# The down product of a two-layer trunk's MLP: eight quarter products feature-major, or seven token-major by Strassen's algorithm

## The chip, the cores and the metric

The kernel runs on one core of one Trainium2 chip. The metric is the device time of one execution in microseconds. Three runs of the kernel before took 1536.81 us (median), from 1536.06 to 1536.86 us.

## The reference

A trunk of two layers works on 512 positions of 1024 features, in float32. Layer 0 mixes the positions by a gated delta rule, layer 1 by a conformer convolution. Each layer then attends to a memory of 256 rows and ends with the MLP that the change concerns:

```
def sq_relu_mlp(h, w_up, w_down):
    return jnp.square(jax.nn.relu(h @ w_up)) @ w_down
```

`h` is the residual stream after `rms_norm` (each row multiplied by 1/rms and by a gain per feature). `w_up` is 1024 x 4096 and `w_down` 4096 x 1024. The result is added to the residual stream. A last `rms_norm` gives the output, 512 x 1024. Since relu is positively homogeneous, multiplying a row of `h` by 1/rms multiplies its row of the hidden activation, after the square, by 1/rms squared.

## The kernel before

Nearly all of its work is dense products on TensorE (PE). A float32 operand is split into a rounded part and the rest, and a product becomes three matmuls: rounded by rounded, rest by rounded, rounded by rest. `mm3` (L229 to L231) issues them. Weights arrive by one queue of SP (`wload`, L196) in tiles of 128 x 1024 called `raw`. `wsplit` makes `wh` by a cast on ACT (L207) and `wl` by a subtraction on DVE (L70 is the line of the helper `tt`, L73 that of `stt`, so that all such operations carry these lines). Those of `w_pw1` and half of layer 1's K and V are subtracted on POOL instead.

The activations lie feature-major: 128 features on the partitions, 512 tokens along a row. So a weight block of 128 x 128 is the stationary operand and 512 tokens move past it. One **unit** makes 128 output features: eight blocks of the inner dimension, three matmuls each, 24 matmuls in one PSUM bank.

The MLP (`mlp`, L960 on) cuts the 4096 hidden rows into four **groups** of 1024 (g = 0 to 3). A group has eight up units and eight down units. `MLP_ORDER` runs them as up 0, up 1, down 0, up 2, down 1, up 3, down 2, down 3, so that a down product never follows directly on its own up product, but for the last. After an up unit, `up_ev` has DVE take relu times 1/rms out of PSUM (`rl`; `rb` is 1/rms spread over the partitions, made by two matmuls, L300), ACT squares it (L970), and ACT and DVE split it (`uh`, `ul`). After a down unit DVE adds the bank to the residual stream (`h`). At the end of layer 0, group 3's additions are followed by the parts of the next norm: ACT multiplies by the gain (`xh`, L314), DVE makes the rest (`xl`), ACT squares, POOL sums the squares.

The last group of layer 1 is made otherwise, in `finish` (L1374 to L1396): token-major, with hidden activations as the stationary operand and 512 columns of weights moving. Four transposes per bank (L1374) bring the residual stream in.

The program is written as one list. A scheduler places each instruction on its engine by its place in that list and by when its inputs and a free tile are expected. The weight tiles come from three pools of three (`raw`, `wh`, `wl`), other wide tiles from pools `fs` and `cv`, and 512-wide tiles from one pool of 69.

Of the kernel before, what the change touches and what calls it, by code (L numbers as in the profile page):

```python
# [11 lines left out]
ALU = mybir.AluOpType  # L12
# [26 lines left out]
def tile_trunk(ctx, tc, xT, memT, prm_d, adt_d, bdw_d, tap_d, fin_d, w_ab, w_kq, w_v, w_z, w_dno, w_pw1, w_pw2,  # L39
# [5 lines left out]
    wp = ctx.enter_context(tc.tile_pool(name="wp", bufs=2))  # L45
    fsp = ctx.enter_context(tc.tile_pool(name="fsp", bufs=3))
# [10 lines left out]
    def slot(dt=F32, s="u", shape=(P, NT)):  # L57
        return up.tile(list(shape), dt, tag="u", name=nm(s))

# [46 lines left out]
    raw0 = wp.tile([P, 1024], F32, tag="raw", name="raw0", bufs=NRAW)  # L106
# [32 lines left out]
    order, srcs = [], {}  # L139

    def plan(key, src, n=2):
        srcs[key] = src
        for hf in range(n):
            order.append((key, hf))
# [14 lines left out]
    def plan_mlp(layer, last=False):  # L159
        for kind, g in MLP_ORDER:  # L160
            if last and (kind, g) == ("dn", 3):
                break
            for i in range(4):
                plan((kind, layer, g * 4 + i), (w_up if kind == "up" else w_dn)[layer, g * 4 + i])
# [11 lines left out]
    for i in range(8):  # L176
        srcs[("pw1", i)] = w_pw1[i]
        srcs[("K", 1, i) if i < 4 else ("V", 1, i - 4)] = w_k[1, i] if i < 4 else w_vv[1, i - 4]
    for kind, i in CONV_SEQ:
        if kind == "p":  # L180
            order.append((("pw1", i // 2), i % 2))
        elif kind == "k":
            order.append((("K", 1, i // 2) if i < 8 else ("V", 1, i // 2 - 4), i % 2))
# [3 lines left out]
    plan_mlp(1, True)  # L187
# [3 lines left out]
    def wload():  # L191
        u = ws["load"]
        key, hf = order[u]
        ws["load"] += 1
        raw = wp.tile([P, 1024], F32, tag="raw", name=nm("raw"), bufs=NRAW)
        nc.sync.dma_start(out=raw, in_=srcs[key][:, hf * 1024:(hf + 1) * 1024])  # L196
        ws["raw"][u] = raw

    def wsplit():
        u = ws["split"]  # L200
        ws["split"] += 1
        while ws["load"] <= u:
            wload()
        raw = ws["raw"].pop(u)
        h = wp.tile([P, 1024], F32R, tag="wh", name=nm("wh"), bufs=NW)
        lo = wp.tile([P, 1024], F32R, tag="wl", name=nm("wl"), bufs=NW)
# [3 lines left out]
        (kind, i, *j), hf = order[u]  # L210
        gp = kind == "pw1" or j and kind in "KV" and i == 1 and hf == 0
        ins.append(tt(pool if gp else dve, lo, raw, h.bitcast(F32), ALU.subtract))
        if u < 4:
            tc.keep_in_program_order(ins[1])
        ws["hl"][u] = (h, lo)

    def wnext(key, hf):
        i = ws["next"]
        assert order[i] == (key, hf), (order[i], key, hf)
        while ws["load"] < min(i + NRAW + 2, len(order)):  # L220
            wload()
        while ws["split"] < min(i + (NW if i else 1), len(order)):
            wsplit()
# [79 lines left out]
    class Norm:  # L303
        def __init__(self, gname, eng=None, two=True):
            self.eng, self.two = eng or pool, two
            self.g, self.acc, self.xs, self.n = gname, None, [], 0
# [5 lines left out]
        def parts(self, t, h):  # L312
# [4 lines left out]
            self.xs.append((xh, xl))  # L317
# [10 lines left out]
        def stat(self):  # L328
# [7 lines left out]
            dve.reciprocal(self.tok, sd)  # L336
            if self.two:
# [21 lines left out]
    class DeltaNet:  # L359
# [109 lines left out]
        def conv_raw(self, ps):  # L469
            raw = wp.tile([P, 542], F32, tag="cv", name=nm("cv"), bufs=NCV)  # L470
# [77 lines left out]
        def fs_in(self, h):  # L548
            gq, bt, n = h // 4, c4(self.BT[h]), h % 4 * 4
            if gq not in self.DB:  # L550
                self.DB[gq] = fsp.tile([P, 1024], F32, tag="fs", name=nm("DB"))
# [6 lines left out]
        def fs_begin(self, gq):  # L558
            X = fsp.tile([P, 1024], F32, tag="fs", name=nm("X"))
            pool.memset(X, 0.0)  # L560
            pool.memset(X[:, 0:1024:33], 1.0)
            FT = fsp.tile([P, 1024], F32, tag="fs", name=nm("FT"))
# [13 lines left out]
        def fs_end(self, gq, i):  # L576
            X = self.fs[gq][-1]
            t = fsp.tile([P, 1024], F32, tag="fs", name=nm("UB" if i == 0 else "TB"))
# [218 lines left out]
    def mem_spread():  # L797
        ps = psum("mrs")
        spread2(ps[:, 0:256], mem.pop("dg"))
        mem["rs"] = slot(s="mrs")  # L800
        act.copy(mem["rs"][:, 0:256], ps[:, 0:256])

    def mem_gain(layer, half):
# [3 lines left out]
        for j in (2 * half, 2 * half + 1):  # L807
            mh = slot(F32R, "mh")
            ml = slot(F32R, "ml")
            for i in range(2):  # L810
# [5 lines left out]
                mem["xs"].append((mh[:, ks], ml[:, ks]))  # L816

# [142 lines left out]
    def mlp(layer, norm, hres, nxt, mid=None, end=None, pre=None):  # L960
        xs = norm.xs
        hid = {}
        cur = list(hres)
        st = {"first": []}

        def up_ev(g, i, ps):
# [562 lines left out]
```

## Time and profile before

| what | value |
| --- | --- |
| median of three runs | 1536.81 us |
| span of the profiled execution | 1533.4 us |
| the profiled execution's own time | its span, 1533.4 us; 3.4 us under the median of the runs |
| PE busy | 1511.9 us (99%) |
| VectorE (DVE) busy | 900.1 us (59%) |
| ScalarE (ACT) busy | 676.3 us (44%) |
| GpSimd (POOL) busy | 228.7 us (15%) |
| HBM read | 149.42 MB |

The profile lists groups of equal instructions as "line engine operation out<-in xcount | busy, mean ns of one | idle time of the engine just before them and what ended it". For a matmul, the first input is the one that moves and the second the stationary one. A row of a stretch gives the busy time of each engine in it, the granted clock of PE and the share of the DMA engines. PE can read as fully busy where its matmuls follow each other closely.

### The profile page before, as it was taken

Reading aid. Unit: us, or ns where it says so; the run is one execution under the profiler, and the core shown is the slowest. Engines: PE = TensorE matmul, PEld = TensorE weight load, DVE = VectorE, ACT = ScalarE, POOL = GpSimd, SP = SyncE. Lnnn points to the kernel's source line nnn. Section 1 sums busy time; section 2 is a strip of 40 time slices with the busy share of each in tenths; the row PEclk is TensorE's granted clock in tenths of the full one; section 3 lists DMA queues with packets and bytes.
Section 4 is the critical chain, followed back from the end, with each engine's and each line's share of the span. In section 5 each row is a group of like instructions: output and inputs, shape, how many; then the busy total and the mean of one; then the engine's idle time right before and its main releaser. Section 6 shows DMA issues by size and latency. Waiting matters only on the chain.

```text
span 1533.4 us, 19367 instructions
## 1 busy us (share of the span) xinstructions
PE 1511.9 (99%) x7560; PEld 1274.0 (83%) x7560; DVE 900.1 (59%) x1372; ACT 676.3 (44%) x1089; POOL 228.7 (15%) x231
## 2 busy tenths in 40 slices
PE   9999999999999999999999999899999999999998
PEld 7888888988888888888888889878888888888886
DVE  6898898766545543443445599864554543434441
ACT  6847655655434442332324464363443441323332
POOL 1421220103112000000003685302112000000000
PEclk9999999999999999999999999999999999999999
DMA  5321123342213222222234524422212222232231
GB/s 179 100 82 62 60 76 111 124 152 82 74 37 110 96 97 97 96 96 97 96 109 150 180 85 149 155 95 96 74 51 97 97 96 97 96 98 97 99 106 55
DMA packets 49051, 153.56 MB, mean 100 GB/s; under 512 B 6208, under 2 KB 8000, under 8 KB 48960
## 3 DMA queue, kind: packets, MB, share of 16 engines
q1 hardware_dynamic: 48960, 152.33, 29.6%
q8 instruction: 59, 0.97, 0.2%
q14 instruction: 32, 0.26, 0.1%
HBM read 149.42 MB, written 2.10 MB: 99 GB/s over the span
## 4 chain that ended last, share of the span: by engine, by line
PE 78%; ACT 1%; DVE 1%; DMA 0%; POOL 0%; issue 0%; ACTq 0%; POOLq 0%; DVEq 0%
PE up L229 8%; PE up L231 8%; PE up L230 8%; PE dn L230 7%; PE dn L231 7%; PE dn L229 7%; PE pw L229 3%; PE pw L231 3%; PE pw L230 3%; PE q L229 2%; PE xo L230 2%; PE q L231 2%; PE q L230 2%; PE xo L229 2%; PE xo L231 2%; PE cv L1130 1%
## 5 line engine op out<-in xcount | busy, mean ns | idle before, releaser
L207 ACT CAST wh<-raw 128x1024 fp32r<-128x1024 f32 x248 | 260.0, 1051 | 627.3 <-PE dn L230 190.4
L70 DVE TENSOR_TENSOR wl<-raw,wh 128x1024 fp32r<-128x1024 f32 x224 | 275.9, 1233 | 96.3 <-ACT wh L207 94.7
L229 PE MATMUL up<-xh,wh 128*128 128x512 f32 x512 | 199.4, 389 | 0.0
L231 PE MATMUL up<-xh,wl 128*128 128x512 f32 x512 | 199.2, 389 | 0.0
L230 PE MATMUL up<-xl,wh 128*128 128x512 f32 x512 | 199.2, 389 | 0.0
L231 PE MATMUL dn<-uh,wl 128*128 128x512 f32 x448 | 174.3, 389 | 0.0
L229 PE MATMUL dn<-uh,wh 128*128 128x512 f32 x448 | 174.3, 389 | 0.0
L230 PE MATMUL dn<-ul,wh 128*128 128x512 f32 x448 | 174.3, 389 | 0.0
L70 DVE TENSOR_TENSOR h<-dn,h 128x512 f32<-128x512 f32 x56 | 41.8, 747 | 163.3 <-PE dn L231 163.3
L73 DVE SCALAR_TENSOR_TENSOR rl<-up,rb 128x512 f32<-128x512 f32 x64 | 44.2, 691 | 153.6 <-PE up L231 153.6
L70 POOL TENSOR_TENSOR sq<-sq,sq 128x512 f32<-128x512 f32 x30 | 48.6, 1621 | 470.1 <-ACT sq L321 470.1
L230 PEld LDWEIGHTS up<-xl,wh 128*128 128x128 f32 x512 | 96.1, 188 | 20.0
L231 PEld LDWEIGHTS up<-xh,wl 128*128 128x128 f32 x512 | 96.1, 188 | 20.0
L229 PEld LDWEIGHTS up<-xh,wh 128*128 128x128 f32 x512 | 96.1, 188 | 20.0
L229 PEld LDWEIGHTS dn<-uh,wh 128*128 128x128 f32 x448 | 84.1, 188 | 17.5
L230 PEld LDWEIGHTS dn<-ul,wh 128*128 128x128 f32 x448 | 84.1, 188 | 17.4
L231 PEld LDWEIGHTS dn<-uh,wl 128*128 128x128 f32 x448 | 84.1, 188 | 17.4
L73 DVE SCALAR_TENSOR_TENSOR ca<-x,prm,ca 128x512 f32<-128x512 f32 x120 | 87.9, 751 | 2.9 <-ACT ca L1093 1.3
L229 PE MATMUL h<-xh,wh 128*128 128x512 f32 x192 | 77.5, 404 | 1.2 <-ACT xh L314 1.2
L230 PE MATMUL h<-xl,wh 128*128 128x512 f32 x192 | 75.5, 393 | 0.6 <-DVE xl L73 0.6
L231 PE MATMUL h<-xh,wl 128*128 128x512 f32 x192 | 75.4, 393 | 0.0
L70 POOL TENSOR_TENSOR wl<-raw,wh 128x1024 fp32r<-128x1024 f32 x24 | 59.1, 2466 | 50.0 <-ACT wh L207 38.2
(348 smaller groups left out, 3068.0 us busy)
## 6 DMA issues: line engine op xcount, KB each, us to landing
raw<-w_up SPq DMA_DIRECT2D x64, 512.0 KB, 3.4
raw<-w_dn SPq DMA_DIRECT2D x64, 512.0 KB, 3.5
raw<-w_pw SPq DMA_DIRECT2D x24, 512.0 KB, 3.6
raw<-w_kq SPq DMA_DIRECT2D x16, 512.0 KB, 3.7
raw<-w_k SPq DMA_DIRECT2D x16, 512.0 KB, 3.8
raw<-w_vv SPq DMA_DIRECT2D x16, 512.0 KB, 3.8
raw<-w_q SPq DMA_DIRECT2D x16, 512.0 KB, 3.5
raw<-w_o SPq DMA_DIRECT2D x16, 512.0 KB, 3.5
```

Of the source, the lines that this page charges most:

```text
L70: return e.tensor_tensor(out=o, in0=a, in1=b, op=op)
L73: dve.scalar_tensor_tensor(out=o, in0=a, scalar=s, in1=b, op0=op0, op1=op1)
L207: ins = [act.copy(h, raw)]
L229: pe.matmul(ps, wh, xh, start=first, stop=False)
L230: pe.matmul(ps, wh, xl, start=False, stop=False)
L231: pe.matmul(ps, wl, xh, start=False, stop=last)
L1130: pe.matmul(o, x, TAPS[m][2 * j + u // 4][:, (u % 4) * P:(u % 4 + 1) * P], start=u == 0, stop=False)
```

## The change

For each group of 1024 hidden rows the down product is seen as a 2 x 2 product of blocks: tokens (2 x 256) by hidden rows (2 x 512), times hidden rows (2 x 512) by output features (2 x 512). It is done by Strassen's algorithm in Winograd's form with seven block products M1 to M7 in place of eight. The change has these parts.

- **Products.** Each block product is 24 matmuls, with the hidden activations as stationary operand and 512 columns of weights, or of differences of weights, moving. The results are token-major. Three pairs of PSUM banks (a, c, b) hold them. Some products add onto what a bank already holds; bank pair b collects M2 of all four groups.
- **Taking results.** After each product but M2 of groups 0 to 2, `take` adds the pair of banks to `y` in SBUF, times 1/rms squared (`rb2`, one number per token): on ACT the first time, else on DVE. Where two products leave a bank for two results, it is taken twice. `up_ev` no longer multiplies by 1/rms, and the two matmuls that spread it are gone (`stat(rb2)`).
- **Sums of operands.** ACT does relu and square. Per pair of up units DVE makes the sums and differences S1 to S4 of hidden activations (128 x 256 each), split by ACT and DVE. Per group DVE makes eight differences of weight tiles of 128 x 1024 (`sub`). Fourteen weight tiles are split for a group's down product in place of eight.
- **Order.** Each up group is followed by its own down product.
- **Ends.** Layer 0 ends by turning `y` with 32 transposes of 128 x 128 (`turn_out`), and `close` adds it to the residual stream and makes the norm's parts. The conformer's first two units are interleaved and take features in the order `K_FIRST`. Layer 1 turns the residual stream into `y` with 32 transposes in its first up group (`turn_in`); those of `finish` are gone. The final norm is in `early` and `late`.
- **Pools and loads.** One pool of 19 tiles of 128 x 1024 replaces `raw`, `wh`, `wl`, `fs` and `cv`. Down weights are loaded during the up units of their group. `mem` is loaded again for layer 1.

The orders below are those of the instructions on one engine; dna, dnb and dnc are tiles of the bank pairs a, b and c.

PE, the start of a down product, before (layer 0). The unit fills one bank with stationary weights (`wh`, `wl`) and moving hidden activations (`uh`, `ul`):

```order
L229 MATMUL dn_6075<-uh_5216,wh_5993 128x512
L230 MATMUL dn_6075<-ul_5218,wh_5993 128x512
L231 MATMUL dn_6075<-uh_5216,wl_5994 128x512
L229 MATMUL dn_6075<-uh_5255,wh_5993 128x512
L230 MATMUL dn_6075<-ul_5257,wh_5993 128x512
```

Now the last up unit is followed at once by M1 of the same group. The weights move, and `al` (both parts of the first 256 tokens of a hidden tile) or `s12h` and `s12l` (both parts of S1 and S2) are stationary:

```order
L279 MATMUL up_5175<-xh_4843,wl_5055 128x512
L1074 MATMUL dna_5231<-wh_5089,al_4891 128x512
L1075 MATMUL dna_5231<-wh_5089,al_4891 128x512
L1076 MATMUL dna_5231<-wl_5090,al_4891 128x512
...
L1074 MATMUL dnc_5271<-wh_5176,s12h_4938 128x512
L1075 MATMUL dnc_5271<-wh_5176,s12l_4940 128x512
L1076 MATMUL dnc_5271<-wl_5177,s12h_4938 128x512
```

The distance between an up product and the down product that uses it went from a whole group to nothing.

DVE in a down product of layer 0, before: an addition of a finished bank and a subtraction for the next weight tile alternate:

```order
L70 TENSOR_TENSOR h_6100<-dn_6075,h_5524 128x512
L70 TENSOR_TENSOR wl_6105<-raw_6030,wh_6104 128x1024
L70 TENSOR_TENSOR h_6133<-dn_6108,h_5557 128x512
L70 TENSOR_TENSOR wl_6138<-raw_6069,wh_6137 128x1024
L70 TENSOR_TENSOR h_6166<-dn_6141,h_5590 128x512
```

Now (group 1) two takes stand for each product, with the weight tiles, the last parts of S3 and S4 and the weight differences (`raw<-raw,raw`) between them:

```order
L75 SCALAR_TENSOR_TENSOR y_5264<-dna_5868,rb_0_4850,y_5264 128x512
L72 TENSOR_TENSOR wl_5932<-raw_5591,wh_5931 128x1024
L72 TENSOR_TENSOR s34l_5854<-s_1240_5839,s34h_5852 128x512
L75 SCALAR_TENSOR_TENSOR y_5301<-dnc_5899,rb_0_4850,y_5301 128x512
L72 TENSOR_TENSOR wl_5948<-raw_5467,wh_5947 128x1024
L75 SCALAR_TENSOR_TENSOR y_5303<-dnc_5906,rb_0_4850,y_5303 128x512
L72 TENSOR_TENSOR wl_5966<-raw_5498,wh_5965 128x1024
L72 TENSOR_TENSOR wl_5982<-raw_5630,wh_5981 128x1024
L75 SCALAR_TENSOR_TENSOR y_5337<-dna_5861,rb_0_4850,y_5337 128x512
L72 TENSOR_TENSOR wl_6001<-raw_5682,wh_6000 128x1024
L75 SCALAR_TENSOR_TENSOR y_5339<-dna_5868,rb_0_4850,y_5339 128x512
L72 TENSOR_TENSOR raw_5453<-raw_5682,raw_5453 128x1024
```

The next product waits for the takes of the bank that it writes, and DVE has about twice as many wide operations there.

DVE at the end of layer 0, before: each down unit's addition and the norm's rest `xl` have a whole unit of PE between them and the next pair:

```order
L70 TENSOR_TENSOR h_7141<-dn_7116,h_6808 128x512
L70 TENSOR_TENSOR wl_7153<-raw_7070,wh_7152 128x1024
L73 SCALAR_TENSOR_TENSOR xl_7145<-h_7141,prm,xh_7143 128x512
L70 TENSOR_TENSOR h_7181<-dn_7156,h_6841 128x512
L73 SCALAR_TENSOR_TENSOR xl_7185<-h_7181,prm,xh_7183 128x512
```

Now the eight additions and rests come in one row, after the takes of M2, with those of M4 (`y_5491`, `y_5493`) among them:

```order
L75 SCALAR_TENSOR_TENSOR y_5262<-dnb_5417,rb_0_4850,y_5262 128x512
L75 SCALAR_TENSOR_TENSOR y_5264<-dnb_5424,rb_0_4850,y_5264 128x512
L72 TENSOR_TENSOR h_7383<-yT_7363,h_4715 128x512
L75 SCALAR_TENSOR_TENSOR xl_7387<-h_7383,prm,xh_7385 128x512
L72 TENSOR_TENSOR h_7391<-yT_7368,h_4757 128x512
L75 SCALAR_TENSOR_TENSOR y_5491<-dna_7127,rb_0_4850,y_5491 128x512
L75 SCALAR_TENSOR_TENSOR xl_7395<-h_7391,prm,xh_7393 128x512
L72 TENSOR_TENSOR h_7400<-yT_7373,h_4799 128x512
L75 SCALAR_TENSOR_TENSOR y_5493<-dna_7134,rb_0_4850,y_5493 128x512
L75 SCALAR_TENSOR_TENSOR xl_7404<-h_7400,prm,xh_7402 128x512
...
L72 TENSOR_TENSOR h_7503<-yT_7468,h_4675 128x512
L75 SCALAR_TENSOR_TENSOR xl_7507<-h_7503,prm,xh_7505 128x512
```

On PE the conformer's units follow directly on the 32 transposes that feed these additions.

The diff, cut to its core:

```diff
+        if name == "M1":
+            return q("11"), lambda: sub("11", "12", "11")
+        if name == "M5":
+            return q("11"), lambda: sub("12", "22", "12")
+        if name == "M6":
+            return sub("11", "22", "11"), None
+        if name == "M3":
+            return drop("22"), None
+        if name == "M7":
+            return drop("12"), None
+        if name == "M2":
+            return q("21"), lambda: (sub("11", "21", "11"), drop("21"))
+        return drop("11"), None
...
-        def up_ev(g, i, ps):
-            t = slot(s="rl")
-            stt(t, ps, 0.0, norm.rb, ALU.max, ALU.mult)
+        def up_ev(i, ps):
             u = slot(s="u2")
-            act.activation(u, t, AF.Square)
-            hid.setdefault(g, []).append(split(u, "u"))
+            act.activation(u, ps, AF.Relu)
+            act.activation(u, u, AF.Square)
...
+            a1, a2, b1, b2 = a[:, 0:256], a[:, 256:512], u[:, 0:256], u[:, 256:512]
+            s12, s34 = slot(s="s12"), slot(s="s34")
+            tt(dve, s12[:, 0:256], a2, b2, ALU.add)
+            bh, bl = split(u, "b")
+            tt(dve, s12[:, 256:512], s12[:, 0:256], a1, ALU.subtract)
+            h, lo = split(s12, "s12")
+            tt(dve, s34[:, 0:256], a1, a2, ALU.subtract)
+            tt(dve, s34[:, 256:512], b1, s12[:, 256:512], ALU.subtract)
+            h, lo = split(s34, "s34")
...
+                    pe.matmul(ps, ah[:, cs], w[hf][0][:, s_], start=fresh, stop=False, skip_group_check=more)
+                    pe.matmul(ps, al[:, cs], w[hf][0][:, s_], start=False, stop=False, skip_group_check=more)
+                    pe.matmul(ps, ah[:, cs], w[hf][1][:, s_], start=False, stop=end, skip_group_check=more)
...
+        def take(bk, tp, i, j):
+            t, ps = 2 * i + tp, bank[bk, tp]
+            sc = rb2[:, t:t + 1]
+            if y[t][j] is None:
+                y[t][j] = slot(s="y")
+                act.activation(y[t][j], ps, AF.Copy, scale=sc)
+            else:
+                stt(y[t][j], ps, sc, y[t][j], ALU.mult, ALU.add)
...
+        def late(t):
+            act.activation(slot(s="fq"), y[t][0], AF.Square, accum_out=ss)
+            act.activation(sd, ss, AF.Sqrt, bias=done[t], scale=1.0 / 1024)
+            dve.reciprocal(rc, sd)
+            act.activation(y[t][1], y[t][1], AF.Copy, scale=rc)
+            stt(y[t][0], y[t][0], rc, gt[:, 0:512], ALU.mult, ALU.mult)
...
+        def close(m):
+            hn = slot(s="h")
+            tt(dve, by_phase(hn), phased(done.pop(m)), phased(hres[m]), ALU.add)
+            nxt.add(m, hn)
...
+            for name in DN_PRODUCTS:
+                bk, form, (oi, oj) = PRODUCT[name]
+                product(g, name, bk, form)
...
+                for tp in range(2):
+                    take(bk, tp, oi, oj)
...
+                elif name == "M2":
+                    turn_out(range(4, 8), range(4))
+                    for m in range(4, 8):
+                        close(m)
+                elif name == "M4":
+                    turn_out(range(4), range(3))
+                    turn_out(range(4), range(3, 4))
+                    for m in range(4):
+                        close(m)
...
+                for k in K_FIRST:
+                    for j in range(2):
+                        mm3(st[0, j], wk(w[j], k), xs[k], k == K_FIRST[0], k == K_FIRST[-1])
...
+NBIG = 19
+DN_PRODUCTS = ("M1", "M5", "M6", "M3", "M7", "M2", "M4")
+PRODUCT = {"M1": ("a", "11", (0, 0)), "M5": ("c", "S1", (1, 1)), "M6": ("a", "S2", (0, 1)), "M3": ("c", "S4", (0, 1)),
+           "M7": ("a", "S3", (1, 1)), "M2": ("b", "12", (0, 0)), "M4": ("a", "22", (1, 0))}
+DN_AHEAD = 3
+NW_DN = 4
+K_FIRST = (4, 5, 6, 7, 0, 1, 2, 3)
-MLP_ORDER = [("up", 0), ("up", 1), ("dn", 0), ("up", 2), ("dn", 1), ("up", 3), ("dn", 2), ("dn", 3)]
```

More of the change, by code (lines that the diff above doesn't have):

```diff
@@ L214, in wsplit @@
             tc.keep_in_program_order(ins[1])
+        if then is not None:
+            then()
         ws["hl"][u] = (h, lo)
@@ L469, in conv_raw @@
         def conv_raw(self, ps):
[L470 removed]
+            raw = big("cv")[:, 0:542]
             pool.memset(raw[:, 0:3], 0.0)
```

305 lines of the change are left out of this document (177 added, 128 removed).

## The prediction

> **What bounds the kernel now.** I read the head of the page first, then the rows by stretch, then the waits of PE.
>
> ```profile
> span 1533.4 us, 19367 instructions
> PE 1511.9 (99%) x7560; PEld 1274.0 (83%) x7560; DVE 900.1 (59%) x1372; ACT 676.3 (44%) x1089; POOL 228.7 (15%) x231
> PE   9999999999999999999999999899999999999998
> ```
>
> PE is idle for 1533.4 − 1511.9 = 21.5 us in all. A busy share can hide slow matmuls, so I need their pitch, and I need it in the MLP. The rows by stretch give time, then busy time and count of PE, weight loads, DVE, ACT and POOL, then the granted clock, the DMA share and GB/s:
>
> ```profile
> 498.35:847.17 348.82, 348.82 (x1541) 288.77 (x1541) 157.17 (x179) 118.91 (x156) 16.50 (x9) 1.00 0.32 104
> 580.00:624.00 44.00, 44.00 (x196) 36.44 (x195) 15.99 (x17) 9.64 (x11) 0.00 (x0) 1.00 0.29 98
> 930.00:970.00 40.00, 40.00 (x327) 39.02 (x326) 39.35 (x78) 14.23 (x25) 16.35 (x10) 1.00 0.51 176
> ```
>
> The first row is nearly the whole MLP of layer 0, from its second unit to the conformer's first: 64 units of 24 matmuls and two matmuls that spread 1/rms.
>
> ```profile
> 503.95 0.47 PE rb L300 x2
> ```
>
> So one matmul takes (348.82 − 0.47) / 1536 = 0.2268 us, at full clock and without a gap. DVE works 157 of 349 us there, ACT 119. In this stage only the number of matmuls counts. In the conformer (third row) DVE is full too (39.35 of 40), which matters at the end of layer 0. PE's longest wait of the whole program is there, for the convolution's taps:
>
> ```profile
> PE cvT L1114 <- ACT ca L1099: 4.7, 1, 4.7
> ```
>
> **The change part by part.** I name T0 the start of a group's down product.
>
> *a. Fewer matmuls.* Each of eight groups has 7 x 24 instead of 8 x 24: −192. The new ones have weights as the moving side. The chain of the last group before has this orientation already:
>
> ```profile
> 1480.22 0.44 PE dn L1374 x4
> 1480.66 0.24 PE dn L1377
> 1486.14 0.44 PE dn L1374 x4
> ```
>
> 24 matmuls in 1486.14 − 1480.66 = 5.48, 0.228 each: the same pitch. −192 x 0.2268 = **−43.5 us**. A new product takes 24 x 0.2268 = 5.44, seven 38.1, a group with its eight up units 81.6.
>
> The Trainium skill ("TensorE: Matmul & The Clock Gate", Back-to-back issue gap) gives about 131 ns per matmul of 512 columns as the sustained figure. By it the part would be worth −25.2 and the sum below would be 18 us higher, 1522. The rows above measure 227 ns here, so the trace disagrees and decides.
>
> *b. No spread of 1/rms* in the two MLPs: four matmuls of 0.47 / 2: **−0.9**.
>
> *c. Transposes.* 32 at layer 0's end are new; the 32 that turn layer 1's residual stream replace those of the last group. The row "x4" above is 0.44, so 32 x 0.11 = **+3.5**.
>
> *d. The end of layer 0.* Before, the eight additions and their norm parts lay one unit apart (5.44 us), and only the last was near the path:
>
> ```profile
> 822.14 0.74 DVE L73 SCALAR_TENSOR_TENSOR xl<-h,prm,xh 128x512 fp32r<-128x512 f32 x1
> 831.83 2.39 POOL L70 TENSOR_TENSOR wl<-raw,wh 128x1024 fp32r<-128x1024 f32 x1 [2.37 <-ACT wh L207]
> 830.88 1.08 DVE L70 TENSOR_TENSOR h<-dn,h 128x512 f32<-128x512 f32 x1 [2.56 <-PE dn L231]
> 832.76 2.02 DVE L73 SCALAR_TENSOR_TENSOR xl<-h,prm,xh 128x512 fp32r<-128x512 f32 x1 [0.79 <-ACT xh L314]
> L73 DVE SCALAR_TENSOR_TENSOR xl<-h,prm,xh x8: 736/756/2016, 811.1 to 843.7; 128x512 fp32r<-128x512 f32 x8
> L314 ACT ACTIVATE xh<-h,prm 128x512 fp32r<-128x512 f32 x40 | 28.9, 722 | 15.9 <-DVE h L70 14.3 <-DVE h L73 1.7
> ```
>
> Now they stand in a row on DVE behind the takes of M2. Each is an addition of 1.08, a wait of 0.79 for ACT's `xh`, and `xl`: 0.75 alone (median of the eight, in the row with least, median and most), 2.02 where POOL has an operation at the same time. So a tile takes 2.7 (rounded up for the hand-overs) to 3.95. The two takes of M4 fit into the waits for `xh`.
>
> PE's side: six products end at T0 + 32.6, then 16 transposes (1.76), M4 (5.44), 16 transposes (1.76). The conformer's first two units, interleaved, need the tiles in the order 4 to 7, 0 to 3, six matmuls (1.36) for each. Unhindered they end at T0 + 41.6 + 8 x 1.36 = 52.5. DVE's side: the first addition can start at about T0 + 33.6 (six products, four transposes, a hand-over and the queued takes partly beside them). Eight tiles of 2.7 end at 55.2, eight of 3.95 at 65.2; the last tile's matmuls that still follow take about 1.1. The stall is 3.8 to 13.8. POOL has two weight tiles of `w_pw1` to subtract there, so I take two blocked `xl` (2 x 1.25): 57.6 + 1.1 − 52.5 = **+6.3**. Nothing takes this back: DVE, full in the conformer, gets its first work from these units.
>
> The Trainium skill ("SBUF — State Buffer", Who interferes with whom) says that a DVE instruction with two SBUF inputs and a GpSimd one that reads SBUF share a read port, and that the later one waits for the whole of the first. The rows agree: `xl` ended at 834.78, 0.56 after POOL's 2.39. By this rule each `xl` could wait for one of POOL's sums of squares as well, and the stall would be near its upper bound, the sum near 1511.
>
> *e. The tail.* After the last matmul there came a square out of PSUM, small operations, one multiplication and the output:
>
> ```profile
> 1527.36 0.24 PE dn L1379
> 1528.94 0.75 DVE y L73
> ```
>
> Now a take (about 0.75) stands before the square, and DVE does another tile's multiplication first: **+1.8**, between 0.8 (the take alone) and 2.6 (two such operations more).
>
> *Costed at nothing, because PE covers it.* The rows for DVE and ACT:
>
> ```profile
> L70 DVE TENSOR_TENSOR wl<-raw,wh 128x1024 fp32r<-128x1024 f32 x224 | 275.9, 1233 | 96.3 <-ACT wh L207 94.7
> L70 DVE TENSOR_TENSOR ul<-u,uh 128x512 fp32r<-128x512 f32 x64 | 44.3, 692 | 5.8 <-ACT uh L266 5.5
> L70 DVE TENSOR_TENSOR fst<-FT,X 128x252 f32<-128x252 f32 x4 | 1.7, 422 | 0.1
> L73 DVE SCALAR_TENSOR_TENSOR h<-pw,prm,h 128x512 f32<-128x512 f32 x8 | 6.0, 750 | 14.7 <-PE pw L231 14.6
> L207 ACT CAST wh<-raw 128x1024 fp32r<-128x1024 f32 x248 | 260.0, 1051 | 627.3 <-PE dn L230 190.4
> L266 ACT CAST uh<-u 128x512 fp32r<-128x512 f32 x64 | 39.8, 622 | 2.1
> L970 ACT ACTIVATE u<-rl 128x512 f32<-128x512 f32 x64 | 40.1, 626 | 9.6 <-DVE rl L73 9.6
> ```
>
> DVE per group: 22 rests and 8 differences of weights, 30 x 1.233 = 37.0; 12 rests of activations, 8.3; 20 quarter tiles at the 252-wide row's 0.42, 8.4; 12 takes like `h<-pw,prm,h` (one input in PSUM), 9.0. Together 62.7 of 81.6. ACT: 22 casts, 23.1, and some 30 operations of 0.62, 18.6, together 42. Neither bounds. The margin is thinner in two places. First, S1 of the last pair of up units is made after the up product that M1 follows at once: relu, square, sum, difference, cast, rest (0.63 + 0.63 + 0.42 + 0.42 + 0.62 + 0.69 = 3.4) and what is queued between them on DVE and ACT, ready at about T0 + 7.2. M5 needs it for its second half at T0 + 5.44 + 2.72 + hand-over, about 9.0. Cover 1.8 us, eight times. Second, four products per group write a bank that a take must have emptied. One product (5.44) lies between, and two takes (1.5) with two weight operations (2.5) fit into it.
>
> Weight loads keep their bytes, but the up phase now carries those of the down product too, two tiles of 0.5 MB in a unit of 5.44: 193 GB/s for three quarters of a phase. The program's start moves 179 at a share of 0.53, so this fits:
>
> ```profile
> 0.00:38.00 38.00, 35.03 (x150) 27.00 (x151) 25.74 (x50) 23.57 (x35) 4.87 (x23) 0.96 0.53 179
> ```
>
> The shared pool also reorders the other stages. Their matmuls are the same, and their idle time is about 13 of the 21.5 us; I take 0, and ±4.
>
> Sum: −43.5 − 0.9 + 3.5 + 6.3 + 1.8 = −32.8. The span goes from 1533.4 to 1500.6. The median of the runs lies 3.4 above the profiled span, so the time is 1536.8 − 32.8 = **1504.0**.
>
> **The rivals.**
>
> *Late S1 in every group.* If ACT or DVE hold that chain behind weight casts (1.05) and rests (1.23), two more of each make it 4.6 late against a cover of 1.8: a stall of about 2.5 on average in each of eight groups, +20, **1524**. For it: the row for `wh` on ACT is long, and the order puts weight subtractions between S1's steps. Against it: by the sums above DVE is idle for a fifth of a group, ACT for half.
>
> *The end of layer 0 without a stall.* If the scheduler's expectations are right and the closes keep pace with PE, part d goes: **1498**. For it: half of the eight `xl` of the boundary before took 0.76 or less. Against it: 8 x 2.7 alone is too long.
>
> *DVE becomes the bound of the MLP* (the slower side). Its 62.7 us per group grow past PE's 81.6 if the 30 operations of 128 x 1024 are stretched, as `xl` was by 2.7 times beside POOL. The gain is gone at 81.6 + 32.8 / 8 = 85.7 per group, which is (85.7 − 25.7) / 30 = 2.0 us for each. At 2.2 it is 91.7, 8 x 6.0 = 48 over that point: **1585**; just past it, 2.03, 1544. For it: 2.39 for the same operation on POOL shows that contention can cost this much. Against it: POOL works 0.00 us between 580 and 624, and the change gives it nothing in the MLP.
>
> *The change does not do what it says.* The order of PE has 1344 matmuls in the down products, 1536 before; so only their pitch could differ, and the 5.48 above speaks against that.
>
> **How the numbers follow.** The forecast has 0.65, with its own range of 1497 to 1513 (d's bounds −2.5 and +7.5, the other stages ±4, e ±1). Late S1 0.15, the end without a stall 0.12, DVE as the bound 0.06, the same matmuls at another pitch 0.02. The range is 1494 to 1522: it takes in the case without a stall less half of the ±4 and late S1 up to 2.2 us per group. A measurement here can tell about 0.2%, 3 us, from no change. The first three cases and most of what is left of the gain elsewhere lie well under 1533: faster 0.92. Same 0.02, slower 0.06, from DVE as the bound.
>
> **What would show it.** PE's matmul groups of the down product should be 1344 in number at a pitch of 0.227, with PE's granted clock at 1.00. In the waits of PE a new row should stand for `pw` on `xl` or `xh` at the end of layer 0, of some 4 to 14 us in all; none of over 1 us for M5 on `s12` or for a product on a take. DVE should be busy some 63 us per group. I am wrong if the MLP's stretch has gaps on PE in each group (late S1 or takes), if the same operations of DVE last much longer than in the rows above, or if the idle time of the other stages grows by more than 4 us.

## The result and the profile after

The changed kernel takes 1515.94 us (median of four runs, 1515.06 to 1520.84), the kernel before 1536.53 us beside it. The ratio is 0.9874, with a 95% interval of 0.9859 to 0.9888: faster by 20.6 us. The forecast was 1504.0, faster by 32.8, with a range of 1494 to 1522. So the sign and the range held, and 12 us of the forecast gain are missing. Two executions, one of the kernel before (1680 us) and one of a version of the changed kernel (1965 us), ran at a granted clock of 0.85 and 0.70 and are left out of all ratios.

The head of the page after has the span, the busy time of each engine, and PE and its clock in 40 slices:

```profile
span 1513.8 us, 19530 instructions
PE 1480.1 (98%) x7396; PEld 1245.2 (82%) x7396; DVE 1089.0 (72%) x1642; ACT 801.1 (53%) x1275; POOL 229.4 (15%) x231
PE   8999999999999999999999999989999999999998
```

PE works 31.8 us less, but it idles 33.7 us where it idled 21.5. To see where, I cut both spans at the same matmuls: the first `q` of layer 0, the first `up`, the end of the conformer's first two units with the norm's sums, the first `up` of layer 1. Each row is a stretch of the kernel before, with its length, the busy time and count of PE, weight loads, DVE, ACT and POOL, the clock, and the DMA:

```profile
0.00:376.83 376.83, 368.52 (x2154) 316.34 (x2155) 308.18 (x577) 231.14 (x408) 72.67 (x136) 1.00 0.31 103
376.83:491.96 115.13, 114.89 (x572) 97.06 (x570) 60.47 (x86) 49.26 (x91) 19.06 (x15) 1.00 0.22 74
491.96:853.56 361.60, 361.60 (x1604) 299.62 (x1603) 163.97 (x188) 123.27 (x161) 18.91 (x10) 1.00 0.32 106
853.56:1173.96 320.40, 313.30 (x1656) 268.44 (x1656) 222.03 (x339) 157.29 (x267) 118.02 (x71) 0.99 0.32 108
1173.96:1533.40 359.44, 353.62 (x1579) 292.50 (x1577) 145.44 (x182) 115.33 (x163) 0.00 (x0) 1.00 0.28 93
```

The same stretches of the kernel after:

```profile
0.00:389.45 389.45, 373.63 (x2154) 319.68 (x2155) 314.75 (x581) 238.06 (x415) 71.41 (x128) 0.98 0.31 106
389.45:504.72 115.27, 114.98 (x572) 97.06 (x570) 58.31 (x85) 48.55 (x91) 18.69 (x15) 1.00 0.25 84
504.72:854.91 350.19, 346.42 (x1537) 286.25 (x1536) 250.09 (x315) 185.22 (x255) 26.53 (x16) 0.99 0.31 106
854.91:1175.67 320.76, 313.70 (x1658) 268.12 (x1658) 228.69 (x347) 156.63 (x267) 112.82 (x73) 0.99 0.34 113
1175.67:1513.80 338.13, 331.34 (x1481) 274.12 (x1479) 237.16 (x314) 172.67 (x247) 0.00 (x0) 0.99 0.26 89
```

| stretch | before | after | difference |
| --- | --- | --- | --- |
| DeltaNet | 376.8 | 389.4 | +12.6 |
| cross attention of layer 0 | 115.1 | 115.3 | +0.1 |
| MLP of layer 0, first two conformer units | 361.6 | 350.2 | −11.4 |
| rest of the conformer, cross attention of layer 1 | 320.4 | 320.8 | +0.4 |
| MLP of layer 1 and the end | 359.4 | 338.1 | −21.3 |

The two MLPs give what the sum said. The loss is in the first row, in a stage in which no matmul was changed: PE has the same 2154 records in both, it idles 7.5 us more, and its busy time grows by 5.1 at a mean clock of 0.98.

**In the DeltaNet stage** DVE inverts a triangular matrix by a long chain of small operations (forward substitution: `fst` and `X`), then transposes and copies the result. DVE before, around the end of that chain:

```profile
106.01 1.22 DVE L70 TENSOR_TENSOR wl<-raw,wh 128x1024 fp32r<-128x1024 f32 x1
111.54 1.22 DVE L70 TENSOR_TENSOR wl<-raw,wh 128x1024 fp32r<-128x1024 f32 x1
114.52 2.10 DVE L579 STREAM_TRANSPOSE TB<-X 128x1024 f32<-128x1024 f32 x1
117.66 5.50 DVE L596 COPY x<-TB 32x128 f32<-32x128 f32 x16
123.80 1.22 DVE L70 TENSOR_TENSOR wl<-raw,wh 128x1024 fp32r<-128x1024 f32 x1
```

The rests of the weight tiles (`wl`) lie inside the chain, about one per unit of PE. After:

```profile
93.97 1.22 DVE L72 TENSOR_TENSOR wl<-raw,wh 128x1024 fp32r<-128x1024 f32 x1
118.35 2.09 DVE L630 STREAM_TRANSPOSE TB<-X 128x1024 f32<-128x1024 f32 x1
121.49 4.51 DVE L647 COPY x<-TB 32x128 f32<-32x128 f32 x16
126.64 1.22 DVE L72 TENSOR_TENSOR wl<-raw,wh 128x1024 fp32r<-128x1024 f32 x1
```

Between 93.97 and 126.64 there is none. They were made earlier, in a bunch, and the next one stands behind the chain and its copies. That one could have been made sooner: the cast that it needs was done at 103.6, and DVE stood idle for 2.15 us before 107.46:

```profile
102.60 1.04 ACT L253 CAST wh<-raw 128x1024 fp32r<-128x1024 f32 x1
107.46 0.69 DVE L72 TENSOR_TENSOR cv<-h,rb 128x512 f32<-128x512 f32 x1 [2.15 <-PE h L279]
```

So its place in DVE's order held it, not its input; whether a free tile was missing when that order was made, the trace does not show. PE runs out of weights, and again at the second inversion. PE of the kernel after, with the idle time and what ended it in brackets:

```profile
127.91 0.80 PE L279 MATMUL h<-xh,wl 128*128 128x512 f32 x1 [3.72 <-DVE wl L72]
128.50 0.63 PE L277 MATMUL h<-xh,wh 128*128 128x512 f32 x1
258.07 0.80 PE L279 MATMUL h<-xh,wl 128*128 128x512 f32 x1 [3.70 <-DVE wl L72]
```

The matmuls behind each wait last 0.63 where others last 0.39, and follow at 0.43 instead of 0.23. The granted clock (the last number but two) was half there:

```profile
128.00:131.00 3.00, 3.00 (x7) 2.39 (x8) 1.91 (x3) 2.96 (x5) 0.01 (x1) 0.51 0.47 142
```

**In the MLP** a whole group of layer 0 has no gap, and lasts what the forecast said, 81.6:

```profile
586.30:667.90 81.60, 81.60 (x361) 67.57 (x361) 57.48 (x73) 41.25 (x56) 0.00 (x0) 1.00 0.30 103
```

DVE has 57.5 us in it, ACT 41.3; forecast were 62.7 and 42. The other groups have up phases of 43.52 and down phases of 38.08 us as well (the first of each MLP has the norm's sums or the transposes on top), so neither S1 nor a take is waited for in them.

**At the end of layer 0**, rows of four engines in order of time:

```profile
832.70 1.05 ACT L253 CAST wh<-raw 128x1024 fp32r<-128x1024 f32 x1 [2.78 <-POOL wl L72]
833.83 2.36 POOL L72 TENSOR_TENSOR wl<-raw,wh 128x1024 fp32r<-128x1024 f32 x1 [1.10 <-ACT wh L253]
834.41 2.33 DVE L75 SCALAR_TENSOR_TENSOR xl<-h,prm,xh 128x512 fp32r<-128x512 f32 x1 [2.34 <-ACT xh L362]
837.63 0.74 DVE L75 SCALAR_TENSOR_TENSOR y<-dna,rb,y 128x512 f32<-128x512 f32 x1
838.43 1.12 PE L1109 MATMUL yT<-ident,y 128*128 128x128 f32 x4 [3.12 <-DVE y L75]
839.77 0.63 PE L278 MATMUL pw<-xl,wh 128*128 128x512 f32 x1
```

A cast of a `w_pw1` tile on ACT waited for a tile that POOL had to give back, and stood ahead of the second `xh`. So DVE stood idle for 2.34 before `xl` (0.79 before most of the others), and `xl` then lasted 2.33 beside POOL. The second take of M4 is queued behind it, and PE's last four transposes wait 3.12 for that take. Twelve matmuls at the slow pitch follow.

**At the end**, the last matmul, the last take and the last multiplication:

```profile
1506.62 0.39 PE L1076 MATMUL dna<-wl,bh 128*128 128x512 f32 x1
1507.54 0.74 DVE L75 SCALAR_TENSOR_TENSOR y<-dna,rb,y 128x512 f32<-128x512 f32 x1
1509.60 0.75 DVE L75 SCALAR_TENSOR_TENSOR y<-y,sm,gt 128x512 f32<-128x512 f32 x1
```

From the last matmul's end to the span's end it is 6.8 us; before it was 5.8.

### The profile page after: what moved, and what is told of

Its sections match the earlier page's. It is cut to its first block, busy times and chain, and to the rows that moved or that the text cites. A ratio compares the mean times of both kernels' runs of the same rounds, so it can differ in the third digit from the quotient of the medians.

```text
span 1513.8 us, 19530 instructions
## 1 busy us (share of the span) xinstructions
PE 1480.1 (98%) x7396; PEld 1245.2 (82%) x7396; DVE 1089.0 (72%) x1642; ACT 801.1 (53%) x1275; POOL 229.4 (15%) x231
## 4 chain that ended last, share of the span: by engine, by line
PE 86%; DVE 8%; issue 3%; ACT 2%; POOL 1%; DMA 0%; SPq 0%; DVEq 0%; POOLq 0%; ACTq 0%
PE up L279 8%; PE up L277 8%; PE up L278 8%; PE dna L1075 4%; PE dna L1074 4%; PE dna L1076 4%; PE pw L278 3%; PE pw L277 3%; PE pw L279 3%; PE q L277 2%; PE xo L278 2%; PE q L278 2%; PE xo L279 2%; PE q L279 2%; PE dnc L1076 2%
## 5 line engine op out<-in xcount | busy, mean ns | idle before, releaser
L72 DVE TENSOR_TENSOR wl<-raw,wh 128x1024 fp32r<-128x1024 f32 x280 | 346.2, 1242 | 189.4 <-ACT wh L253 88.8
L253 ACT CAST wh<-raw 128x1024 fp32r<-128x1024 f32 x304 | 316.2, 1049 | 283.6 <-PE dna L1075 55.8
L72 POOL TENSOR_TENSOR wl<-raw,wh 128x1024 fp32r<-128x1024 f32 x24 | 61.8, 2583 | 359.4 <-ACT wh L253 342.4
L72 DVE TENSOR_TENSOR raw<-raw,raw 128x1024 f32<-128x1024 f32 x64 | 78.1, 1220 | 0.9
L1031 ACT ACTIVATE u<-up 128x512 f32<-128x512 f32 x64 | 38.1, 596 | 67.1 <-PE up L279 67.1
L75 DVE SCALAR_TENSOR_TENSOR y<-dna,rb,y 128x512 f32<-128x512 f32 x58 | 43.0, 745 | 20.2 <-PE dna L1076 20.0
L75 DVE SCALAR_TENSOR_TENSOR cva<-cv,prm,cva 128x512 f32<-128x512 f32 x60 | 47.7, 813 | 9.0 <-POOL cva L72 7.5
L277 PE MATMUL pw<-xh,wh 128*128 128x512 f32 x128 | 51.2, 402 | 0.3 <-ACT xh L362 0.3
L278 PE MATMUL pw<-xl,wh 128*128 128x512 f32 x128 | 51.0, 398 | 0.3 <-DVE xl L75 0.3
L75 DVE SCALAR_TENSOR_TENSOR xl<-h,prm,xh 128x512 fp32r<-128x512 f32 x40 | 36.1, 902 | 20.7 <-ACT xh L362 20.6
L279 PEld LDWEIGHTS h<-xh,wl 128*128 128x128 f32 x192 | 37.4, 195 | 16.3 <-DVE wl L72 8.3
```

Source lines behind the costliest of these rows:

```text
L72: return e.tensor_tensor(out=o, in0=a, in1=b, op=op)
L75: dve.scalar_tensor_tensor(out=o, in0=a, scalar=s, in1=b, op0=op0, op1=op1)
L253: ins = [act.copy(h, raw)]
L277: pe.matmul(ps, wh, xh, start=first, stop=False)
L278: pe.matmul(ps, wh, xl, start=False, stop=False)
L279: pe.matmul(ps, wl, xh, start=False, stop=last)
```

## The experiments

Times are medians. The ratio to the kernel before is taken on the same chip, with its 95% interval.

### One pool of 19 in the kernel before

Theory P: the shared pool makes the DeltaNet stage longer, because it lifts the limit of three tiles each for `wh` and `wl`. Rival Q: something else in the change does.

```diff
-        h = wp.tile([P, 1024], F32R, tag="wh", name=nm("wh"), bufs=NW)
-        lo = wp.tile([P, 1024], F32R, tag="wl", name=nm("wl"), bufs=NW)
+        h = big("wh", F32R)
+        lo = big("wl", F32R)
```

and the same for `raw`, `fs` and `cv`. As in the changed kernel, the pool of 512-wide tiles has 68 in place of 69, and a scratch area for DMA is smaller.

> The kernel before with only its pools changed: raw, wh, wl, fs and cv tiles all come from one pool of 19, NSLOT 68, the small DMA scratch. Theory P (the shared pool is what made the DeltaNet stage longer: with no limit of three wh and wl tiles the weight rests go to DVE in a bunch ahead of the forward substitution and none lies inside it): the first q matmul moves from 376.8 to about 389, PE waits twice some 3.7 us for wl of h, and the time is about 1536.5 + 12.6 = 1549. Rival Q (the longer stage comes from something else in the change, such as the order of loads or the later program's weight on the scheduler): 1537 within 2.

Measured: 1551.75 us, ratio 1.0099 (1.0082 to 1.0116). The first `q` stands at 392.7. The longest row of PE's waits (total, times, longest):

```profile
PE h L233 <- DVE wl L72: 7.6, 2, 3.8
```

Theory P holds. With the MLP of before untouched, the merged pool brings the same two waits, and costs 15.7 us.

### The weight parts in pools of their own

The changed kernel, with four tiles each for `wh` and `wl`, and 11 for all others:

```diff
-        h = big("wh", F32R)
-        lo = big("wl", F32R)
+        h = wp.tile([P, 1024], F32R, tag="wh", name=nm("wh"), bufs=NW_DN)
+        lo = wp.tile([P, 1024], F32R, tag="wl", name=nm("wl"), bufs=NW_DN)
...
-NBIG = 19
+NBIG = 11
```

> The changed kernel with wh and wl in pools of four each and the other 11 wide tiles shared. Theory P: the rests are paced by PE again, some lie inside the forward substitution on DVE, the two waits of 3.7 us and the matmuls slowed behind them go, and most of the 12.6 us comes back: 1503 to 1506, first q matmul at 377 to 380. Rival Q: 1516, first q at 389. Rival S (fs, cv and raw sharing 11 tiles is itself too tight): no gain, with loads that come late.

Measured: 1499.42 us, ratio 0.9765 (0.9750 to 0.9779). DVE has rests of weights inside the chain again, the last one just ahead of its end:

```profile
113.59 1.22 DVE L72 TENSOR_TENSOR wl<-raw,wh 128x1024 fp32r<-128x1024 f32 x1
115.68 2.10 DVE L630 STREAM_TRANSPOSE TB<-X 128x1024 f32<-128x1024 f32 x1
```

and the stage is:

```profile
0.00:379.10 379.10, 369.08 (x2154) 316.36 (x2155) 311.46 (x577) 230.24 (x407) 68.88 (x128) 1.00 0.34 115
```

10.3 of the 12.6 us are back, and PE's clock is 1.00. Another 3.8 us are won in the conformer and 1.7 at the end of layer 0, which theory P had not named. This is the best version of the study, 16.5 us under the changed kernel. Run again later:

> The run with weight pools of their own once more on the same chip, as the best version so far: 1499.4 within 0.5.

1500.13 us, ratio 0.9767 (0.9752 to 0.9782): 0.2 us more than the forecast allowed.

### Weight tiles merged, with no more room

Is it the mixing of the three kinds, or the room? The kernel before, with `raw`, `wh` and `wl` in one pool of nine:

```diff
-        h = wp.tile([P, 1024], F32R, tag="wh", name=nm("wh"), bufs=NW)
+        h = wp.tile([P, 1024], F32R, tag="w9", name=nm("wh"), bufs=9)
```

and so for `wl` and `raw`.

> The kernel before with raw, wh and wl in one pool of nine, fs and cv as they were. If mixing the three kinds of weight tiles is what unbalances DVE's order in the DeltaNet stage: 1545 or more. If it is the room (weight tiles run ahead only where the tiles of fs and cv are there for them too): 1536.5 within 2, since nine tiles hold the same three units.

Measured: 1530.00 us, ratio 0.9967 (0.9955 to 0.9979). The DeltaNet stage is as before (first `q` at 376.9), so mixing the three kinds does no harm there. What is left is the room that the merged pool gives, or that `fs` and `cv` tiles share it; a larger pool for weight tiles alone was not tried. The 5.3 us that it wins, against either expectation, lie in the conformer; PE's wait for the taps there, 4.7 before and followed by slow matmuls, is now followed by none and is

```profile
PE cvT L1114 <- ACT ca L1099: 2.0, 1, 2.0
```

### What a wait costs PE

The version with weight pools of its own, with six waits put into PE, each behind fills on POOL:

```diff
+                if g and i == 3:
+                    st_ = slot(s="stall")
+                    pool.tensor_copy(st_[:, 0:128], u[:, 0:128])
+                    for _ in range(STALL[3 * layer + g - 1]):
+                        pool.memset(st_, 0.0)
+                    tc.keep_in_program_order(pe.transpose(psum("stall")[:, 0:P], st_[:, 0:P], ident))
```

> As the run with weight pools of their own, with six waits put into PE between the fourth and fifth up unit of groups 1 to 3 of both layers: PE must wait for the unit's relu and square and then for 0, 2, 3, 4, 6 and 9 fills on POOL (0.53 each), so for about 1.8, 2.9, 3.4, 3.9, 5.0 and 6.6 us. If a wait costs only itself: 1499.4 + 23.6 = 1523. If waits of some 3 us and more are followed by matmuls at a pitch of 0.43 instead of 0.227, as after the two waits of 3.7: those of 3.4 and up cost 1.3 to 2.8 each on top, 1529 to 1534, and none behind 1.8.

Measured: 1544.83 us, one run with its profile. The waits came out longer than planned, 30.0 us in all where 23.6 were meant, so the time lies above both sums; with 30.0, waits that cost only themselves would give 1529.4. The first two, with a matmul behind them:

```profile
603.23 0.33 PE L1134 MATMUL stall<-ident,stall 128*128 128x128 f32 x1 [2.67 <-POOL stall L1131]
604.33 0.39 PE L278 MATMUL up<-xl,wh 128*128 128x512 f32 x1
...
689.05 0.33 PE L1134 MATMUL stall<-ident,stall 128*128 128x128 f32 x1 [3.84 <-POOL stall L1133]
690.72 0.63 PE L277 MATMUL up<-xh,wh 128*128 128x512 f32 x1
```

The granted clock was 0.50 behind the second, and 1.00 behind the first:

```profile
690.70:693.70 3.00, 3.00 (x8) 2.30 (x7) 0.69 (x1) 0.14 (x1) 0.00 (x0) 0.50 0.00 0
604.00:608.00 4.00, 4.00 (x20) 3.26 (x19) 2.13 (x5) 0.76 (x2) 0.00 (x0) 1.00 0.35 116
```

An up phase lasts 43.52 us without a wait, so each wait's whole price can be read from its phase:

| wait, us | up phase, us | price | beyond the wait | slow matmuls |
| --- | --- | --- | --- | --- |
| 2.67 | 46.57 | 3.05 | 0.4 | 0 |
| 3.84 | 49.35 | 5.83 | 2.0 | 8 |
| 4.42 | 50.89 | 7.37 | 3.0 | 12 |
| 5.00 | 50.47 | 6.95 | 2.0 | 8 |
| 6.17 | 52.86 | 9.34 | 3.2 | 13 |
| 7.91 | 54.33 | 10.81 | 2.9 | 12 |

The second theory's pattern holds: the short wait costs itself and 0.4 us, those of 3.8 and more cost 2 to 3 us besides, whatever their length. The slow stretch begins a while after the wait (1.3 us after the one of 3.84) and lasts 3 to 6 us, at 0.427 per matmul, 1.88 times the pitch of 0.227. The Trainium skill ("TensorE: Matmul & The Clock Gate", Part 1: The HAM clock gate) says that PE falls to half its rate after an idle window of about 3.4 us, that it takes about one such busy window to come back, and that the windows run free of the kernel, so that the count of slow matmuls varies. The trace agrees: none behind 2.67, 8 to 13 behind 3.84 and more. Eight slow matmuls are 3.4 us; 12 and 13 are over 5, longer than one such window. Where PE had other waits or transposes shortly before, shorter waits were followed by slow matmuls too: one of 1.81 by five in the run with four units below, and one of 1.50 behind transposes by six in the run with POOL off, by none in this version without the six waits.

### Strassen's algorithm undone

The version with weight pools of its own, with the classical eight block products instead of seven, token-major all the same:

```diff
-DN_PRODUCTS = ("M1", "M5", "M6", "M3", "M7", "M2", "M4")
+DN_PRODUCTS = ("C1", "C2", "C3", "C4", "C5", "C6", "C7", "C8")
...
-            tt(dve, s12[:, 0:256], a2, b2, ALU.add)
-            tt(dve, s12[:, 256:512], s12[:, 0:256], a1, ALU.subtract)
...
+            h, lo = split(u, "b")
```

> As the run with weight pools of their own, but the down product token-major by the classical eight block products (no sums of activations, no differences of weights, 16 weight tiles split per group, 8 takes), so 24 more matmuls per group. If the number of matmuls alone sets the MLP: 1499.4 + 192 x 0.2268 = 1543, within 3. If Strassen's extra work on DVE and ACT costs something that I do not see (DVE falls to some 45 us per group here), less: under 1538.

Measured: 1544.23 us, ratio 1.0063 (1.0046 to 1.0080), 44.8 us more than with Strassen's seven. The MLPs grow by 21.7 and 21.3 us, 43.0 together. A stretch inside the MLP:

```profile
600.00:760.00 160.00, 160.00 (x708) 132.53 (x707) 76.79 (x76) 71.45 (x87) 0.00 (x0) 1.00 0.29 95
```

DVE has 76.8 of 160 us to do here. The 192 matmuls are worth 43.5 by their pitch, so they are the whole of the gain, and the sums and differences cost nothing that can be seen in the MLP. Token-major by itself, without Strassen, is slower than the kernel before even with the better pools.

### DVE loaded to the brim

The changed kernel, each weight rest of a down product made twice:

```diff
         ins.append(tt(pool if gp else dve, lo, raw, h.bitcast(F32), ALU.subtract))
+        if kind == "dn":
+            tt(dve, lo, raw, h.bitcast(F32), ALU.subtract)
```

> The changed kernel with each of the 14 weight rests of a group's down product made twice on DVE: 17.3 us more per group, 62.7 + 17.3 = 80.0 of the 81.6 us that PE needs, with all of the addition in the down phase (28.5 + 17.3 = 45.8 on DVE against 38.1 of PE). If the sum over a whole group decides (DVE may run ahead in the up phase): no more than 1 us per group, 1516 to 1524. If the down phase decides by itself, since its rests can't be made before tiles are free: 45.8 - 38.1 = 7.7 us in each of eight groups, about 1516 + 62 = 1578.

Measured: 1534.79 us, ratio 0.9995 (0.9986 to 1.0004); 18.9 us over the changed kernel, between the two expectations. Inside the MLP, and around the end of layer 0:

```profile
600.00:760.00 160.00, 159.52 (x703) 131.37 (x702) 142.50 (x173) 76.20 (x105) 0.00 (x0) 1.00 0.30 98
780.00:870.00 90.00, 79.49 (x336) 59.86 (x335) 82.36 (x94) 41.89 (x63) 29.75 (x17) 0.94 0.36 114
```

With DVE 89% busy a down phase lasts 38.66 instead of 38.08: the sum over the group decides there, as the first theory said. But from the first up unit to the norm's sums layer 0 loses 12.7 us, of which its first three groups have 1.4, and layer 1 loses 6.1 with 1.2 in three groups. DVE arrives at each end with weight rests left over, for which PE waits 3.9 us in the second stretch, and the closes or the last takes stand behind them. So the forecast's rival "DVE becomes the bound" bites first at the ends: the kernel is as slow as the one before with DVE at 142.5 of 160 us, 72.7 per group, not at 85.7.

### The end of layer 0

Four runs on the version with weight pools of its own. **Early turn:** features 512 to 1023 are turned and closed ahead of M2.

```diff
+                if name == "M2" and g == 3 and not last:
+                    turn_out(range(4, 8), range(4))
+                    for m in range(4, 8):
+                        close(m)
                 product(g, name, bk, form)
```

> As e2, and at the end of layer 0 the turning and closing of features 512 to 1023 stands ahead of M2 in the program instead of behind it. If the stall of 7.4 us there is made by eight closes in a row on DVE that start too late, starting four of them one product (5.44) earlier takes 5 to 7 us off: 1497 to 1500, and the wait for the last transposes (3.1) goes. If it is made by POOL blocking xl, or by ACT's queue, the closes are as slow earlier and less than 3 us go.

Measured: 1499.55 us, ratio 0.9766 (0.9751 to 0.9780). The wait for the transposes is 1.3 at most, but the weight pools of their own had already brought it from 3.1 to 1.0. The stretch from the first up unit to the norm's sums is 345.5 us in its profile, 347.7 without the early turn (349.4 in the changed kernel). That is 2.2 us in one profile, and the times do not show it. Again:

> The run with the early turn once more, on the same chip as the four interleaved units, for the comparison: 1499.5, from 1497 to 1502.

1499.4 us, ratio 0.9762 (0.9749 to 0.9775). The expected 5 to 7 us are not there. PE's waits for the transposes, `xl` and `xh` are only 3.7 us in all on this version without the early turn, and 2.3 with it, so that much was not there to be won.

**POOL off:** as the early turn, with the first four `w_pw1` rests on DVE.

```diff
-        gp = kind == "pw1" or j and kind in "KV" and i == 1 and hf == 0
+        gp = kind == "pw1" and i > 1 or j and kind in "KV" and i == 1 and hf == 0
```

> As the run with the early turn, and the rests of the first four weight tiles of w_pw1 are made on DVE instead of POOL. If what is left of the stall at the end of layer 0 (3.5 us by the profile) comes from POOL holding up xl, the mean of the eight xl there falls from about 1.2 to below 1.0 and 1 to 3 us go: 1495 to 1498. If DVE's own row of closes sets it, the four rests of 1.23 come on top and the time rises by up to 5 us.

Measured: 1499.20 us, ratio 0.9765 (0.9751 to 0.9780). The eight `xl` (least, median, most):

```profile
L75 DVE SCALAR_TENSOR_TENSOR xl<-h,prm,xh x8: 735/752/753, 815.0 to 837.7; 128x512 fp32r<-128x512 f32 x8
```

None is held up any more (2287 was the longest with the early turn alone), and nothing is won: the stretch is 345.7. The 1 to 3 us of the first expectation did not come, and a rise, as in the second, does not show. The shorter `xl` and the four rests of 1.23 that DVE now makes may cancel, so this run does not show whether POOL or DVE's own row of closes sets the end.

**Four units:** as the early turn, with the conformer's first four units interleaved, so that PE has as much to do per tile as DVE. The edit also splits the weights of these units less far ahead.

```diff
-        nw = NW_DN if key[0] in ("up", "dn") else NW
+        nw = 1 if key[0] == "pw1" and key[1] < 2 else NW_DN if key[0] in ("up", "dn") else NW
...
-                w = [wnext(("pw1", 0), j) for j in range(2)]
+                w = [wnext(("pw1", j // 2), j % 2) for j in range(4)]
```

> As the run with the early turn, and the conformer's first four units instead of two are interleaved, so that PE has 12 matmuls (2.72 us) for each closed tile, as much as DVE needs for a close (2.7 to 3.1). If the rest of the stall (3.5 us) is DVE's row of closes against six matmuls (1.36) per tile, it goes down to 1 us or less: 1496 to 1498. But the first four products are then finished together, 10.9 us of PE work later than the first pair was: if DVE, full in the conformer, starts late on them, what is won is lost there again, and the conformer's stage grows by as much: 1499 or more.

Measured: 1512.67 us, ratio 0.9847 (0.9834 to 0.9861): 13 us worse. PE waits for no `xl` or `xh` at the end of layer 0, so the closes are hidden, as the first theory said. But now

```profile
PE pw L279 <- POOL wl L72: 2.2, 2, 1.8
PE rb L348 <- DVE dg L72: 8.2, 1, 8.2
838.00:860.00 22.00, 15.70 (x74) 13.06 (x72) 6.59 (x6) 4.14 (x5) 8.14 (x5) 0.90 0.13 41
```

The first is for weight rests on POOL that are made later now. In the second PE has nothing while the norm's statistics are made, and DVE has 6.6 of 22 us to do where the early turn has 14.0. Neither expectation had the wait of 8.2.

**Four units, late spread:** the spread behind the fifth unit.

```diff
-                if (m, hf) == (1, 0):
+                if (m, hf) == (2, 0):
                     norm.spread()
```

> As the run with four interleaved units, with the two matmuls that spread 1/rms of that norm behind the fifth unit instead of right behind the four, so that PE has 5.4 us of work while the norm's statistics are made (they took 8.2 us there with PE waiting). If that wait was the only loss: the 8.2 us and what its slow matmuls cost go, except 2 to 3 us that the fifth unit does not cover, and the first part of the theory (four units hide the closes) can be read from PE's waits for xl and xh: 1498 to 1503. If the conformer, where DVE is full, loses by getting its first tiles 10 us later: 1506 or more.

Measured: 1518.42 us, ratio 0.9889 (0.9872 to 0.9905). The wait for `dg` shrinks, and new ones come at the end of the conformer, where DVE is late:

```profile
PE cvT L1278 <- ACT ca L1263: 5.3, 1, 5.3
PE V L309 <- DVE wl L72: 4.8, 1, 4.8
PE rb L348 <- DVE dg L72: 4.6, 2, 2.5
```

So the second expectation holds. It fits a conformer in which DVE is the bound, so that what counts is when it gets its first tile: hiding the closes behind more PE work gives that tile to it later. The later weight rests on POOL are in both runs, and were not tried by themselves.

## Why the prediction was right, and where it was not

The large term was right for its reason. That the time lies in the stated range is in part luck: 1515.94 is outside the forecast's own 1497 to 1513, and inside 1494 to 1522 by the room that was there for late S1, which did not happen. One of the forecast's own signs of being wrong came true: the idle time of the other stages grew by 7.5 us, over its limit of 4.

- **a, fewer matmuls, and b:** right. Each MLP gave its 22.2 us. Undoing Strassen alone costs 43.0 in the MLPs, against 43.5 by the sum. A group lasted 81.6 us to the tenth.
- **c:** the 32 transposes lie where the order had them. They and d are 10.8 together (−11.4 against −22.2), 9.8 in the sum; the split between them is not measured by itself.
- **d, the end of layer 0:** +7.3, if c is taken as 3.5; +6.3 forecast, 3.8 to 13.8 as bounds (its 57.6 is 57.7 when added up). Size and engine were right, the path was not: the waits of `pw` for `xl` and `xh`, forecast at 4 to 14, are 0.6 in all. The long wait, 3.1, is for the take of M4 behind a late `xl`, and a part of the price is PE's slow matmuls, which the sum did not have. POOL held up `xl` as forecast (2.33 beside its 2.36), but with POOL's rests taken away nothing is won.
- **e, the tail:** +1.0 for +1.8, between its bounds.
- **Costed at nothing in the MLP:** right, with margin. No wait for S1 or a take is in any group of the changed kernel, so the rival "late S1" fell; DVE loaded to 89% cost 0.6 us per group. The forecast read POOL's 2.39 as a sign of contention; it is POOL's usual time for that operation (median of 24 in the kernel before: 2.40, least 2.38).
- **Costed at nothing in the other stages:** wrong, and this is the missing gain. "The shared pool also reorders the other stages ... I take 0, and ±4" measured +13.1, of which +12.6 in the DeltaNet stage. Two waits of 3.7 us, each with slow matmuls behind it, are the larger part. The forecast counted matmuls there and idle time (15.6 us by the stretches above, not its 13), and did not ask what paced the weight rests. It was the three tiles each of `wh` and `wl`: a full pool holds a split back until PE has used an older one. With 19 shared tiles the rests were made in a bunch, and the scheduler placed the next one behind DVE's chain. The pool put into the kernel before costs 15.7 us, and taken from the changed kernel gives 16.5, of which 10.3 in this stage. That the splits used the room of `cv` and `fs` is the likely reason for the bunch, but no run shows it alone.
- **The price of a wait** was taken as its length. From 3.8 us on it is 2 to 3 us more.

What stays open: why the best version's DeltaNet stage is still 2.3 us longer than before (3.3 in its second profile), what sets the end of layer 0 there, and whether the early turn's 2.2 us are real.

## What to carry to other kernels

A change of tile pools is a change of schedule for every stage that shares them: here a small pool was also a throttle that spread work evenly over a long chain on another engine. When an edit merges pools, look at the order of the busiest side engine in all stages, not only in the one that is rewritten. And where the engine that feeds PE is nearly full, look at the ends of a phase first: a sum over the whole phase may fit while the last results queue behind leftovers.

## What the runs showed of the hardware that was not expected

A wait of PE can have two prices. In a row of matmuls without other waits, the wait of 2.67 us cost about itself, and those of 3.84 us and more were followed by 8 to 13 matmuls at 0.427 us instead of 0.227, at a granted clock of 0.50. Length alone does not decide: in the changed kernel the wait of 3.12 at the end of layer 0 was followed by 12 such matmuls too, with 12 transposes of 128 x 128 just ahead of it, and one of 2.42 in front of four transposes in the conformer by seven. Whether transposes keep the clock up less than matmuls do was not tried.
